# Seven-product chunks and the delays of deferred work set place by place, and the softmax reciprocal moved to the attended rows, in a hybrid decoder layer

## The chip, the cores and the metric

The kernel runs on one core of a Trainium2 chip. The metric is the device time of one execution in microseconds, and lower is better. The core has a matrix engine (TensorE, PE in the profile, with its weight loads as PEld), a vector engine (DVE), a scalar engine (ACT), GpSimd (POOL) and a synchronisation engine (SP), whose queue here issues nearly all DMAs.

## The reference

One decoder layer on 256 tokens of width 2048, in float32 (SEQ = 256, D_MODEL = 2048, N_MEM = 256, D_FF = 5632, 4 attention heads of 512):

```
hn = rmsnorm(h, norm_mix_w)
q, k, v, g_ret, xr, yr, g_a, g_b = split(hn @ w_in)
ret_out = silu(g_ret) * head_groupnorm(retention(rotary(q), rotary(k), v))
rnn_out = gelu(yr) * rg_lru(causal_dwconv(xr))
merged = sigmoid(g_a) * (ret_out @ w_proj_ret) + sigmoid(g_b) * (rnn_out @ w_proj_rnn)
h = h + merged @ w_mix_out
q = rmsnorm(h, norm_xa_w) @ xa_w_q;  k, v = mem_n @ xa_w_k, mem_n @ xa_w_v
h = h + (softmax(q k^T / sqrt(512)) v) @ xa_w_o              # per head
gate, val = split(causal_dwconv(rmsnorm(h, norm_ffn_w) @ w_up))
h = h + (silu(gate) * val) @ w_down
out = rmsnorm(h, final_norm_w)
```

Nearly all of the arithmetic lies in the weight products: a [256, K] activation times a [K, 512] block of columns, K being 2048 for most.

## The kernel before

**Weights.** `weight_plan` lists the weight products in their order. An entry is either one block of 512 columns or a pair of such blocks; a pair carries its own tuple from MARKS. `weight_stream` cuts them into chunks: a single block of 2048 rows has four chunks of 4 x 128 rows, a pair has eight chunks of 2 x 128 rows for both blocks. Each chunk is one 1 MB load into one of three `raw` buffers (RAW_BUFS), issued on SP. The chunks of a pair are numbered 0 to 7 here.

**Three products for one.** To hold float32 accuracy, every matrix is split into a high part and the rest. `weight_parts` does it for weights: ACT copies raw to `hi` (L355), DVE subtracts to `lo` (L356). Activations are split likewise (`split_pair`, `split_cols`). One product of 128x128x512 is then three matmuls, high x high, low x high and high x low. There are six buffers for each of hi and lo (PART_BUFS), and a tile holds two blocks of 128x512; a seven-product chunk takes four tiles of each, a plain pair chunk two. `chunks` runs `prefetch(AHEAD)`, so loads and splits are listed two chunks before the matmuls that use them.

**Seven products for eight.** A plain pair chunk multiplies a 2 x 2 arrangement (two halves of the tokens by two blocks of rows, two blocks of rows by two blocks of columns): eight block products, 24 matmuls. At the chunk positions named in MARKS the pair instead forms sums of the weight blocks (`seven_parts`, four additions on DVE, L376) and of the activations (`sums_of`, L454 to L465, kept for later products of the same activations until `token_sums` is cleared), and needs seven block products, 21 matmuls. Every pair has at least one such position before the change, mostly 2 and 5.

**Pair ends.** `steps_pair` accumulates in two acc and two sm banks of PSUM, in three more bank pairs for the seven-product chunks, and DVE adds them up at the end (L529, L540).

**Deferred work.** `later(n, fn)` puts fn into a list; `chunks` runs it n + 1 chunks on, after that chunk's matmuls have been listed. This is how the work between products gets its place: the transposes, rotary, retention, recurrence, softmax, convolutions, activation splits. `by_dma` turns rows into feature-major form: ACT copies the words to two planes (L562), SP issues transposing DMAs, and `join`, put off by `wait` chunks, copies the result back (L575) and calls `then`, which splits it for its reader.

**Order.** Matmuls stay in program order (`tc.keep_in_program_order`). For the other engines a scheduler at build time orders what is ready by its place in the program; `tc.high_priority(FREE)` moves evacuations of PSUM forward. So a later place in the program gives a lower rank behind weight splits.

**The order of products.** Retention: q, k, v and gates for four heads, twice (the gates as pairs, the second V as a pair). Recurrence: eight single products of w_in, then GB and w_proj_rnn, GA and w_proj_ret, w_mix_out. Attention: xa_w_k (two single blocks), two pairs of xa_w_q, a pair of xa_w_k, xa_w_v and xa_w_o (a pair and two single blocks each). Feed-forward: eleven blocks of w_up, each a pair of gate and value columns, in groups of 4, 4 and 3, with w_down of a group after the first block of the next one.

**Attention.** `softmax` takes the maximum, runs Exp with a summed output, and multiplies the probabilities by the reciprocal of the sum (L1090); `by_dma` turns them. `attend` multiplies by V, and `turned_rows` copies the result from PSUM (L586) for the next turn; with a scale r it multiplies instead (L588).

```python
def later(n, fn):
    pending.append((step[0] + n + 1, fn))
...
by_dma(rows, then, wait=1, pin=False)        # join put off by `wait` chunks
```

The functions that the change touches follow, with the line numbers that the profile uses.

Of the kernel before, what the change touches and what calls it, by code (L numbers as in the profile page):

```python
# [17 lines left out]
P = 128  # L18
# [10 lines left out]
BW = 512  # L29
# [7 lines left out]
RG_WAIT = 3  # L37
# [44 lines left out]
def weight_plan():  # L82
# [13 lines left out]
    plan += [("xa_w_k", 0, NT, 0), ("xa_w_k", 0, NT, BW), both("xa_w_q", 0), both("xa_w_q", 2 * BW), both("xa_w_k", 2 * BW)]  # L96
    plan += [both("xa_w_v", 0)] + [("xa_w_v", 0, NT, b * BW) for b in (2, 3)]
    plan += [both("xa_w_o", 0)] + [("xa_w_o", 0, NT, b * BW) for b in (2, 3)]
# [7 lines left out]
    marks = iter(one for stage in MARKS for one in stage)  # L106
    return [(*p[:3], (*p[3], next(marks)) if isinstance(p[3], tuple) else p[3]) for p in plan]


def marks_of(w, row=0):  # L110

    return next(c[2] for one, r, _, c in weight_plan() if (one, r) == (w, row) and isinstance(c, tuple))
# [59 lines left out]
def hybrid_layer(  # L172
# [308 lines left out]
    def steps_pair(w, row, st, nk, c1, c2):  # L481
# [15 lines left out]
        for k0, n, parts in chunks(nk, w, row, (c1, c2, seven)):  # L497
            k2 = k0 // KH
            for i in seven:
                if k2 < i <= k2 + 3 and (not isinstance(st, list) or i < len(st)):  # L500
                    sums_of(st[i])
# [42 lines left out]

    def product(o, l, r, start, stop):
# [33 lines left out]

    def turned_rows(a, r, then, wait=1, urgent=True):  # L580

        rows = big([P, 2, BW], s="rows")
        with tc.high_priority(FREE) if urgent else nullcontext():
            for tt in range(2):
                if r is None:
                    dve.tensor_copy(rows[:, tt, :], a[:, tt, :])  # L586
                else:
                    dve.tensor_scalar_mul(rows[:, tt, :], a[:, tt, :], r[:, tt : tt + 1])  # L588
# [169 lines left out]
    def retain(g, qr, kr, vs, dec, gates):  # L758
# [36 lines left out]
        def normalise():  # L795
# [18 lines left out]
            for i in range(2):  # L814
                later(2 * i, lambda i=i: two_heads(i))
# [107 lines left out]
    for b in range(4):  # L923
# [6 lines left out]
        def conv_x(f, b=b, xr=xr, wparts=wparts):  # L930
# [18 lines left out]
            for pr in range(2):  # L949
                later(RG_WAIT + pr, lambda pr=pr: both(pr))  # L950
# [10 lines left out]
        turned_rows(gemm_n("w_in", 0, xs, NT, O_YR + b * BW), rs0, gelu_y, 6)  # L961
# [25 lines left out]
    def turn_merged(f):  # L987
        for pr in range(2):
# [3 lines left out]
            if len(merged) == NT // 2:  # L992
                for i, k2 in enumerate(sorted(set(more) - set(marks))):
                    later(1 + i, lambda k2=k2: sums_of(merged[k2]))
            if len(merged) == 2:
                for k2 in range(NT // 2):
                    later(1 + 3 * k2, lambda k2=k2: ms[k2])

    ts, mb = [], []
    for b in range(2):  # L1000
        ts.append(tanh_rows(big([P, 2, BW], s="sig"), gemm_n("w_in", 0, xs, NT, O_GB + b * BW)))
        if b == 0:
            for i, k2 in enumerate(marks_of("w_proj_rnn")):
                later(1 + 2 * i, lambda k2=k2: sums_of(rnn[k2]))
# [14 lines left out]
    for b in range(4):  # L1019
        later(8 + b, lambda b=b: hrow.append(load_rows(x, b)))  # L1020
    for b in (0, 2):
        for i, m in enumerate(pair("w_proj_ret", 0, ret, NT, b * BW, (b + 1) * BW)):
            gated(ts[b + i], m)
            dve.tensor_add(m, m, mb[b + i])  # L1024
            by_dma(m, turn_merged, 1 + (b + i == 3))


    def residual(w, st, out, wcol, paired, marks):

        ss = sums()  # L1030
        products = [steps_n(w, 0, st, NT, b * BW) for b in range(4)]
        sources = []
        for b in range(4):
            if b in paired:
                sources += pair(w, 0, st, NT, b * BW, (b + 1) * BW)
            h = hrow[b]
            dve.tensor_add(h, h, sources.pop(0) if sources else ended(products[b]))
            by_dma(h, lambda f, b=b: turn(f, b, out, wcol, marks), 1 + (b % 2 if b in (*paired, *(i + 1 for i in paired)) else 0), b == 3 and w == "xa_w_o")
            if b < 2:
                later(2 + b, lambda h=h, b=b: squares(h, ss, b))  # L1040
# [20 lines left out]
    ss1 = residual("w_mix_out", merged, h1s, p_xa, (0, 2), ())  # L1061
# [5 lines left out]
    pTs, probs = [], []  # L1067
# [276 lines left out]
```

## Time and profile before

| quantity | value |
|---|---|
| median of 3 runs | 1971.8 us (1971.18 to 1973.38) |
| profiled execution | 1971.99 us, span 1970.2 us |
| TensorE matmuls | 8768, busy 1953.4 us (99%) |
| weight loads | busy 1618.3 us (82%) |
| DVE | 2190 instructions, busy 1653.1 us (84%) |
| ACT | 1729 instructions, busy 1417.8 us (72%) |
| weight loads by DMA | 352 of 1 MB, 4.9 us each from issue to landing |
| granted TensorE clock | 0.998 mean |

The profile is one execution. A stretch is given as start:end in us from the start of the span. "DVE lo L356" is the DVE instruction of line 356 that writes a tile `lo`; "A <- B" in a list of waits says that A was idle until B had ended. Busy times of an engine overlap with those of the others. Ends of matmuls are modelled, so their starts and counts say more than their busy share.

### The profile page before, as it was taken

What the parts mean: (1) busy time and instruction counts of PE and PEld (TensorE: products, weight loads), DVE (VectorE), ACT (ScalarE), POOL (GpSimd) and SP (SyncE); (2) the same over time, 40 slices, a digit from 0 to 9 for tenths busy, and PEclk for the clock granted to TensorE, in tenths of its full rate; (3) what the DMA queues carried; (4) which work ended last, traced back from release to release, by engine and by line L of the source; (5) the groups of instructions that cost most, each with busy time, mean ns of one, the idle gap of its engine ahead of it and who ended that gap; (6) DMA issues with size and microseconds to landing.
All of it is one profiled execution on the core that took longest, in us unless ns stands there. A gap on an engine that the chain in (4) does not pass through costs nothing.

```text
span 1970.2 us, 24139 instructions
## 1 busy us (share of the span) xinstructions
PE 1953.4 (99%) x8768; PEld 1618.3 (82%) x8768; DVE 1653.1 (84%) x2190; ACT 1417.8 (72%) x1729; POOL 31.9 (2%) x33
## 2 busy tenths in 40 slices
PE   9999999999999999999999999999999999999998
PEld 7888888888888888878888888888877888878887
DVE  6887987888798887997888767789999889998786
ACT  6666658999645666778678676888886578874783
POOL 0000001000000000000000000000000000000000
PEclk9999999999999999999999999999999999999999
DMA  8756567765555576678676656667667756767673
GB/s 333 241 214 168 191 244 211 213 224 193 194 213 191 192 262 231 225 237 255 210 212 216 208 176 211 219 210 227 211 208 226 268 195 219 230 209 256 219 245 119
DMA packets 198344, 429.82 MB, mean 218 GB/s; under 512 B 142160, under 2 KB 146768, under 8 KB 153168
## 3 DMA queue, kind: packets, MB, share of 16 engines
q1 hardware_dynamic: 197072, 424.09, 64.4%
q0 software_dynamic: 1152, 4.19, 1.1%
q8 instruction: 68, 1.11, 0.2%
q14 instruction: 52, 0.43, 0.1%
HBM read 388.39 MB, written 2.10 MB: 198 GB/s over the span
## 4 chain that ended last, share of the span: by engine, by line
PE 81%; DVE 10%; ACT 5%; issue 2%; DMA 2%; SPq 0%; POOL 0%; POOLq 0%; ACTq 0%; DVEq 0%
PE acc L257 56%; PE sm L257 24%; DVE lo L356 4%; ACT f L575 2%; ACT hi L355 2%; DMA raw<-in_wall 2%; DVE raw L376 1%; DVE fv L1158 1%; DVE o L540 1%; DVE o L529 1%; DVE s L596 0%; DMA pt<-pl 0%; DVE fo L1167 0%; ACT fg L1156 0%; ACT pl L562 0%
## 5 line engine op out<-in xcount | busy, mean ns | idle before, releaser
L356 DVE TENSOR_TENSOR lo<-raw,hi 128x1024 fp32r<-128x1024 f32 (+1 forms) x838 | 969.4, 1184 | 231.8 <-ACT hi L355 223.2
L355 ACT CAST hi<-raw 128x1024 fp32r<-128x1024 f32 (+1 forms) x838 | 824.3, 1014 | 391.0 <-DVE raw L376 108.0
L257 PE MATMUL acc<-hi,s 128*128 128x512 f32 (+1 forms) x3548 | 1087.3, 388 | 0.7 <-ACT hi L355 0.3
L257 PEld LDWEIGHTS acc<-hi,s 128*128 128x128 f32 x3548 | 663.2, 188 | 137.2 <-ACT hi L355 0.8
L257 PE MATMUL acc<-lo,s 128*128 128x512 f32 (+1 forms) x1774 | 687.4, 388 | 0.0
L257 PE MATMUL sm<-hi,s 128*128 128x512 f32 x1552 | 477.9, 389 | 0.0
L257 PEld LDWEIGHTS acc<-lo,s 128*128 128x128 f32 x1774 | 333.1, 188 | 68.7 <-DVE lo L356 0.4
L257 PEld LDWEIGHTS sm<-hi,s 128*128 128x128 f32 x1552 | 291.3, 188 | 60.6
L257 PE MATMUL sm<-lo,s 128*128 128x512 f32 x776 | 302.0, 389 | 0.0
L575 ACT COPY f<-pt 128x1024 uint16<-128x1024 uint16 x128 | 167.8, 1356 | 15.7 <-DMA pt<-pl 15.5
L376 DVE TENSOR_TENSOR raw<-raw 128x512 f32<-128x512 f32 x248 | 171.2, 690 | 4.3
L257 PEld LDWEIGHTS sm<-lo,s 128*128 128x128 f32 x776 | 145.7, 188 | 30.4 <-DVE lo L356 0.4
L257 PE MATMUL acc<-hi,ts 128*128 128x512 f32 x372 | 115.1, 390 | 1.2 <-ACT hi L355 1.2
L257 PEld LDWEIGHTS acc<-hi,ts 128*128 128x128 f32 x372 | 69.5, 188 | 16.6 <-ACT hi L355 2.6
L257 PE MATMUL acc<-lo,ts 128*128 128x512 f32 x186 | 73.8, 397 | 5.2 <-DVE lo L356 5.1
L562 ACT COPY pl<-o 128x1024 uint16<-128x1024 uint16 x64 | 62.2, 1040 | 5.9 <-DVE o L1024 5.2
L562 ACT COPY pl<-rows 128x1024 uint16<-128x1024 uint16 x44 | 43.8, 1042 | 17.7 <-DVE rows L586 10.3
L257 PEld LDWEIGHTS acc<-lo,ts 128*128 128x128 f32 x186 | 34.9, 188 | 17.0 <-DVE lo L356 10.2
L1158 DVE SCALAR_TENSOR_TENSOR fv<-f,pf,fv 128x255 f32<-128x255 f32 (+1 forms) x88 | 41.5, 483 | 3.3 <-ACT fv L1156 3.0
L529 DVE TENSOR_TENSOR o<-o,acc 128x512 f32<-128x512 f32 x64 | 43.7, 683 | 0.1
L540 DVE TENSOR_TENSOR o<-o,sm 128x512 f32<-128x512 f32 x64 | 42.7, 686 | 0.2
L540 DVE TENSOR_TENSOR o<-o,acc 128x512 f32<-128x512 f32 x64 | 41.1, 685 | 0.9 <-PE acc L257 0.8
(185 smaller groups left out, 1056.8 us busy)
## 6 DMA issues: line engine op xcount, KB each, us to landing
raw<-in_wall SPq DMA_DIRECT2D x352, 1024.0 KB, 4.9
nat<-in_x SPq DMA_DIRECT2D x8, 512.0 KB, 10.6
nat<-o POOLq DMA_DIRECT2D x8, 512.0 KB, 6.3
raw<-in_wall SPq DMA_DIRECT2D x7, 512.0 KB, 5.9
pt<-pl SPq DMA_TRANSPOSE x128, 3.3
nat<-in_mem SPq DMA_DIRECT2D x4, 512.0 KB, 6.8
xt<-in_x_t SPq DMA_DIRECT2D x3, 512.0 KB, 9.1
xt<-in_mem_t SPq DMA_DIRECT2D x3, 512.0 KB, 6.4
```

Of the source, the lines that this page charges most:

```text
L257: tc.keep_in_program_order(pe.matmul(*a, **k))
L355: act.copy(hi[:, cs], src[:, cs])
L356: dve.tensor_tensor(out=lo[:, cs], in0=src[:, cs], in1=hi[:, cs].bitcast(F32), op=ALU.subtract)
L376: dve.tensor_tensor(out=o, in0=a, in1=b, op=ALU.add)
L529: dve.tensor_tensor(out=o, in0=a, in1=b, op=op)
L540: dve.tensor_tensor(out=o, in0=o, in1=banks[a], op=ALU.add)
L562: act.copy(planes[:, tt], words[:, tt])
L575: act.copy(halves_[:, :, :, cs], turned_[:, :, :, cs])
L1158: dve.scalar_tensor_tensor(out=y[:, s:S], in0=z[:, j, 0 : S - s], scalar=pf[:, 2 - s, t : t + 1], in1=y[:, s:S], op0=ALU.mult, op1=ALU.add,)
```

## The change

It has three parts.

1. MARKS gets its own tuple for each pair. An empty tuple now makes `weight_plan` list two single blocks, which is how the first xa_w_k, the last xa_w_v and the last xa_w_o products stay single; `paired()` lets the code below ask which it is. The tuples name one to three chunk positions, among them neighbours such as (2, 5, 6).
2. LAG names the delay of each kind of deferred work. Some values are those of before (recur, two_heads, gelu, value), others differ: rnn 0 for 1, heads 7 for 4, squares 5 in steps of 1 for 6 in steps of 2, rows 12 for 8, merged 2 for 1, memory 3 for 1, merge_turn 2 for 1, turn 3 for 1, query_turn 3 and key_turn 4 for 1, attend 1 for 0, residual 3 for 2, gate 2 for 1. The two accumulating DMAs (acc_m, acc_h) are off at 0.
3. `softmax` leaves the probabilities unscaled and keeps the reciprocals in `shares`; `attend` gives them to `turned_rows`, which multiplies the attended rows on their way out of PSUM.

```diff
+LAG = dict(
+    sums=3, two_heads=2, recur=3, gelu=6, merged=2, memory=3, memory_step=3, rnn=0, rnn_step=2,
+    heads=7, heads_step=1, squares=5, squares_step=1, rows=12, rows_step=1, residual=3, gate=2,
+    value=4, merge_turn=2, query_turn=3, key_turn=4, turn=3, attend=1, acc_m=0, acc_h=0,
+)
...
 MARKS = [
-    ((2, 5), (5,), (2, 5)),
-    ((2, 5), (2, 5), (2, 5)),
-    ((2, 5), (2, 5), (2, 5), (2, 5)),
-    ((5,), (3, 5)),
-    ((2, 5), (2, 5), (2, 5), (2, 5)),
-    ((3, 5),),
-    ((2, 5), (2, 5), (2, 5), (2, 5), (2, 5), (2, 5), (2, 5)),
-    ((2, 5), (2, 5), (2, 5), (2, 5), (2, 5), (2, 5)),
-    ((2, 5), (2, 5)),
+    ((2, 5, 6), (3,), (3, 5, 6),),
+    ((2, 5), (2, 5, 6), (2, 5, 6),),
+    ((2, 4, 6), (2, 5), (2, 5), (5,),),
+    ((3,), (3, 5),),
+    ((), (2, 5), (2, 3), (2, 5), (2, 5), (),),
+    ((5, 6), (),),
+    ((2, 4), (2, 5), (5,), (2, 5), (2, 5), (2, 5), (2, 5),),
+    ((2, 3, 5), (5,), (2, 5), (2, 5), (2, 5), (2, 5),),
+    ((2, 5, 6), (3, 5),),
 ]
...
+            seven = next(marks)
+            out += [(w, row, nk, (*c, seven))] if seven else [(w, row, nk, one) for one in c]
...
         rows = big([P, 2, BW], s="rows")
             for tt in range(2):
-                if r is None:
-                    dve.tensor_copy(rows[:, tt, :], a[:, tt, :])
-                else:
-                    dve.tensor_scalar_mul(rows[:, tt, :], a[:, tt, :], r[:, tt : tt + 1])
+                dve.tensor_scalar_mul(rows[:, tt, :], a[:, tt, :], r[:, tt : tt + 1])
...
-                    later(1 + i, lambda k2=k2: sums_of(merged[k2]))
+                    later(LAG["merged"] + i, lambda k2=k2: sums_of(merged[k2]))
...
-                    later(1 + 3 * k2, lambda k2=k2: ms[k2])
+                    later(LAG["memory"] + LAG["memory_step"] * k2, lambda k2=k2: ms[k2])
...
-    later(4 + h, lambda h=h: split_head(h))
+    later(LAG["heads"] + LAG["heads_step"] * h, lambda h=h: split_head(h))
...
-    later(6 + 2 * c, lambda c=c: memory_squares(c))
+    later(LAG["squares"] + LAG["squares_step"] * c, lambda c=c: memory_squares(c))
...
-    later(8 + b, lambda b=b: hrow.append(load_rows(x, b)))
+    later(LAG["rows"] + LAG["rows_step"] * b, lambda b=b: hrow.append(load_rows(x, b)))
...
-            by_dma(m, turn_merged, 1 + (b + i == 3))
+            by_dma(m, turn_merged, LAG["merge_turn"] + (b + i == 3))
...
-            by_dma(h, lambda f, b=b: turn(f, b, out, wcol, marks), 1 + (b % 2 if b in (*paired, *(i + 1 for i in paired)) else 0), b == 3 and w == "xa_w_o")
+            by_dma(h, lambda f, b=b: turn(f, b, out, wcol, marks), LAG["turn"] + (b % 2 if two else 0), b == 3 and w == "xa_w_o")
...
         dve.reciprocal(rsm, sm)
-        for tt in range(2):
-            dve.tensor_scalar_mul(pr_[:, tt, :], pr_[:, tt, :], rsm[:, tt : tt + 1])
+        shares.append(rsm)
...
-            by_dma(a, lambda f, o=o: split_block(f, o), 1 + i)
+            by_dma(a, lambda f, o=o: split_block(f, o), LAG["key_turn" if w == "xa_w_k" else "query_turn"] + i)
...
-        turned_rows(a, None, lambda f: split_block(f, osp, marks_of("xa_w_o")))
+        turned_rows(a, shares[b], lambda f: split_block(f, osp, marks_of("xa_w_o")))
...
-        later(b, lambda b=b, v=v: attend(b, v))
+        later(LAG["attend"] + b, lambda b=b, v=v: attend(b, v))
...
-        for a, then, wait in zip(two, (gate, value), (1, wait)):
+        for a, then, wait in zip(two, (gate, value), (LAG["gate"], wait)):
```

More of the change, by code (lines that the diff above doesn't have):

```diff
@@ L36 @@
 FREE = 300
-RG_WAIT = 3
+LAG = dict(
[3 more added lines that the diff above has]
+)
 EPS = 1e-6
@@ L105, in weight_plan @@
             plan.append(both("ffn_w_up", a[0] * BW, apart=FF))
-    marks = iter(one for stage in MARKS for one in stage)
-    return [(*p[:3], (*p[3], next(marks)) if isinstance(p[3], tuple) else p[3]) for p in plan]
+    marks, out = iter(one for stage in MARKS for one in stage), []
+    for w, row, nk, c in plan:
+        if isinstance(c, tuple):
+            seven = next(marks)
+            out += [(w, row, nk, (*c, seven))] if seven else [(w, row, nk, one) for one in c]
+        else:
+            out.append((w, row, nk, c))
+    return out
 def marks_of(w, row=0):
-    return next(c[2] for one, r, _, c in weight_plan() if (one, r) == (w, row) and isinstance(c, tuple))
+    return next((c[2] for one, r, _, c in weight_plan() if (one, r) == (w, row) and isinstance(c, tuple)), ())
 def gate_up_at():
@@ L578, in by_dma, with scaled @@
         later(wait, join)
+    def scaled(a, r):
+        with tc.high_priority(FREE):
+            for tt in range(2):
+                act.mul(a[:, tt, :], a[:, tt, :], r[:, tt : tt + 1])
     def turned_rows(a, r, then, wait=1, urgent=True):
@@ L949, in conv_x @@
             for pr in range(2):
-                later(RG_WAIT + pr, lambda pr=pr: both(pr))
+                later(LAG["recur"] + pr, lambda pr=pr: both(pr))
         def gelu_y(f, xr=xr):
```

71 lines of the change are left out of this document (42 added, 29 removed).

## The prediction

> **What bounds the kernel now.** I read the page's engine shares first, then the busy time in stretches that begin with the first matmul of one weight product and end with the first of the next, then the waits, then the groups by form.
>
> ```profile
> span 1970.2 us, 24139 instructions
> PE 1953.4 (99%) x8768; PEld 1618.3 (82%) x8768; DVE 1653.1 (84%) x2190; ACT 1417.8 (72%) x1729; POOL 31.9 (2%) x33
> ```
>
> ```profile
> 500.00:600.00 100.00, 100.00 (x443) 82.81 (x442) 85.29 (x104) 55.85 (x62) 0.00 (x0) 1.00 0.51 190
> ```
>
> TensorE is the bound: in an undisturbed 100 us it starts 443 matmuls, so one costs 100/443 = 0.226 us. Time can go only by fewer matmuls or by removing the few places where TensorE waits. A product of eight chunks with two seven-product chunks has 8x24 - 2x3 = 186 matmuls, or 186 x 0.226 = 42.0 us; undisturbed ones below measure 42.2, and 42.8 with one such chunk. Anything longer is waiting. (Columns: stretch, length, then busy us of PE, PEld, DVE, ACT, POOL.)
>
> ```profile
> 92.90:135.10 42.20, 42.20 (x187) 34.82 (x186) 39.48 (x50) 23.75 (x27) 0.00 (x0) 1.00 0.60 215
> 185.90:230.10 44.20, 43.60 (x190) 35.21 (x189) 39.63 (x64) 34.72 (x40) 0.00 (x0) 1.00 0.71 214
> 230.10:272.30 42.20, 42.20 (x188) 34.96 (x187) 38.95 (x53) 22.81 (x27) 0.00 (x0) 1.00 0.59 218
> 550.90:593.10 42.20, 42.20 (x188) 34.95 (x187) 37.83 (x47) 22.48 (x26) 0.00 (x0) 1.00 0.55 199
> 593.10:635.20 42.10, 42.10 (x187) 34.87 (x186) 33.43 (x39) 22.46 (x26) 0.00 (x0) 1.00 0.55 198
> 635.20:677.40 42.20, 42.20 (x188) 34.93 (x187) 35.92 (x44) 23.25 (x28) 0.00 (x0) 1.00 0.50 186
> 761.70:805.20 43.50, 42.67 (x188) 34.79 (x187) 37.32 (x46) 31.72 (x38) 0.00 (x0) 1.00 0.72 243
> 805.20:848.00 42.80, 42.80 (x190) 35.44 (x189) 38.83 (x50) 31.76 (x39) 0.00 (x0) 1.00 0.73 245
> 848.00:892.70 44.70, 42.77 (x187) 34.76 (x186) 41.66 (x56) 35.66 (x51) 0.00 (x0) 1.00 0.66 214
> 1384.10:1426.90 42.80, 42.49 (x188) 34.85 (x187) 41.40 (x59) 36.86 (x46) 0.00 (x0) 1.00 0.65 221
> 1426.90:1470.60 43.70, 42.59 (x187) 34.66 (x186) 41.64 (x60) 38.33 (x48) 0.00 (x0) 1.00 0.67 217
> 1470.60:1514.60 44.00, 43.39 (x188) 34.54 (x187) 40.74 (x58) 35.39 (x44) 0.00 (x0) 1.00 0.69 215
> 1556.70:1598.90 42.20, 42.20 (x187) 34.92 (x187) 33.22 (x37) 21.62 (x24) 1.07 (x2) 1.00 0.69 232
> 1725.40:1769.00 43.60, 42.59 (x187) 34.74 (x186) 40.49 (x57) 36.38 (x46) 0.00 (x0) 1.00 0.71 217
> 1811.20:1853.40 42.20, 42.20 (x188) 34.95 (x187) 32.91 (x37) 21.64 (x24) 0.88 (x1) 1.00 0.67 226
> ```
>
> The losses are 44.2 - 42.8 = 1.4 (second V product), 43.5 - 42.2 = 1.3 (w_proj_ret, second pair), 44.7 - 42.2 = 2.5 (w_mix_out, second pair), 0.6 + 1.5 + 1.8 = 3.9 (blocks 3 and 4 of w_up, first w_down) and 1.4 (second w_down). Together 10.5 us. In the long ones DVE is busy for nearly all of it (41.64 of 43.7); in the two quiet ones it idles 9 us. So the deferred work on DVE, beside the weight splitting, sets these waits. The waits of the weight load agree:
>
> ```profile
> PEld acc L257 <- DVE lo L356: 10.6, 14, 1.5
> PEld acc L257 <- ACT hi L355: 3.3, 5, 1.6
> ...
> PEld sm L257 <- DVE o L540: 0.7, 1, 0.7
> PEld acc L257 <- DVE ps L1120: 0.7, 1, 0.7
> ```
>
> TensorE waits for the low parts of split weights, and twice in the attention stage for something else (at most 1.4 us together).
>
> **What a seven-product chunk and a token sum cost.**
>
> ```profile
> L356 DVE TENSOR_TENSOR lo<-raw,hi 128x1024 fp32r<-128x1024 f32 x770 | 926.1, 1227 | 230.3 <-ACT hi L355 221.7 <-PE acc L257 3.5
> L376 DVE TENSOR_TENSOR raw<-raw 128x512 f32<-128x512 f32 x248 | 171.2, 690 | 4.3
> L356 DVE TENSOR_TENSOR lo<-raw,hi 128x512 fp32r<-128x512 f32 x68 | 46.5, 688 | 1.5 <-ACT hi L355 1.5
> L454 DVE TENSOR_TENSOR g<-s 128x512 f32<-128x512 f32 x16 | 11.0, 687 | 0.1
> L460 DVE TENSOR_TENSOR tq<-g 128x256 f32<-128x256 f32 x16 | 6.8, 423 | 0.2
> L462 DVE TENSOR_TENSOR tq<-g,tq 128x128 f32<-128x128 f32 x16 | 4.6, 289 | 0.1
> L465 DVE TENSOR_TENSOR ts<-tq,ts 128x512 fp32r<-128x512 f32 x22 | 15.2, 689 | 1.4 <-ACT ts L464 1.4
> L586 DVE COPY rows<-acc 128x512 f32<-128x512 f32 x8 | 5.1, 685 | 1.2 <-PE acc L257 1.0
> L588 DVE TENSOR_SCALAR rows<-acc,ro 128x512 f32<-128x512 f32 x28 | 19.7, 744 | 5.1 <-PE acc L257 5.1
> L1090 DVE TENSOR_SCALAR prob<-prob,sx 128x256 f32<-128x256 f32 x8 | 2.5, 351 | 0.1
> ```
>
> ```profile
> L355 ACT CAST hi<-raw 128x1024 fp32r<-128x1024 f32 x770 | 785.1, 1049 | 372.7 <-DVE raw L376 108.0 <-PE sm L257 105.8 <-DMA raw<-in_wall 78.3
> ```
>
> A plain pair chunk takes 2 x 1.227 = 2.45 us of DVE and 24 matmuls, a seven-product one 4 x 0.690 + 3 x 1.227 + 0.688 = 7.13 us and 21. So each buys 3 x 0.226 = 0.68 us of TensorE for 4.68 us of DVE. The 248 additions of L376 are four each: 62 such chunks. Counted from the new MARKS there are 66. A chunk position that is new for its activations also needs a token sum: 0.687 + 0.423 + 2 x 0.289 (L462 and its twin) + 0.689 = 2.38 us of DVE. There are 22 (L465); the new places make 31.
>
> **The change part by part**, against the profiled execution (1971.99 us, its span and 1.8 around it; 0.2 above the median of the runs shown).
>
> 1. Matmuls: 4 more such chunks remove 12, 12 x 0.226 = **-2.7 us**. (The Trainium skill, "TensorE: Matmul & The Clock Gate", Back-to-back issue gap, gives about 131 ns per matmul of this width when weight loads are pipelined with them: 1.6 us instead, as an estimate. The trace's spacing of 226 ns disagrees, and decides.)
>
> 2. Second half of the mixer: the second w_proj_ret product loses chunk 2, the first w_mix_out product moves its one from chunk 5 to 3, and the turns and splits of merged and memory tiles come one to two chunks later, which takes DVE work out of 848.0 to 892.7. DVE gains 4.68 us against a loss of 1.3 + 2.5 = 3.8.
>
> ```profile
> ACT hi L355 <- DMA raw<-in_wall: 5.6, 4, 2.9
> ```
>
> But in 848.0 to 892.7 the casts also wait 5.6 us for weights, whose issue queues on SP behind other transfers, and the loads of x rows now come four chunks later past weight loads on that queue (still a whole product ahead of their first reader). I take **-2.8** (0 to -3.8).
>
> 3. First feed-forward half: block 2 of w_up drops chunk 2, just ahead of the 3.9 us lost. DVE gains 4.68, TensorE's own time there grows by 0.68, one token sum (new chunk 4 in block 0) takes 2.38 back: net 2.98 of lead. **-3.0** (0 to -3.9).
>
> ```profile
> L575 ACT COPY f<-pt 128x1024 uint16<-128x1024 uint16 x128 | 167.8, 1356 | 15.7 <-DMA pt<-pl 15.5
> ```
>
> The last turn of xa_w_o is joined two chunks later, with two chunks left to its reader (21 + 24 matmuls, 10.2 us). Ahead of that reader stand on ACT its two copies, 2.7 us, and at most six casts of 1.049 for the weights of those chunks, 6.3: 9.0 in all, with its own splits behind. It just fits: 0, at most +2, once. Gate joins one chunk later; its reader waits for value anyway: 0.
>
> 4. Second half: block 6 drops chunk 2; block 5 gains one with a sum, 7.06 us, where 42.2 - 33.2 = 9.0 us are idle. The 1.4 us go: **-1.4** (0 to -1.4).
>
> 5. Second V product: its chunk moves from 5 to 3 and asks a new sum, 2.38 us, in a stretch already short. **-0.4** (-1.4 to +2.4).
>
> 6. Attention: probabilities lose 8 x 0.351 = 2.8 us, attended rows pay 8 x (0.744 - 0.685) = 0.5 on DVE; attend, keys and queries come one to three chunks later. The attended rows wait for a reciprocal finished many chunks before. Of the 1.4 us I take **-0.5** (-1.4 to +1.4, as much again).
>
> 7. Added chunks, extra DVE against idle DVE: 92.9: 7.06 to 2.7; 230.1: 4.68 to 3.3 (sums made before); 550.9: 7.06 to 4.4; 593.1: 7.06 to 8.7; 635.2: 7.06 to 6.3; 1811.2: 7.06 to 9.3. Short are 4.4 + 1.4 + 2.7 + 0.8 = 9.3 us, which must come out of the lead that the splitting has. That lead shows where casts wait for TensorE to free a part buffer, here in 593.1 to 635.2 and in 92.9 to 135.1:
>
> ```profile
> ACT hi L355 <- PE sm L257: 10.0, 8, 1.7
> ```
>
> ```profile
> ACT hi L355 <- PE sm L257: 4.7, 4, 1.7
> ```
>
> As long as they wait, splitting is as far ahead as six buffers allow. So nearly all is covered: **+0.7** (0 to 9.3), nearer the first end because no such wait of TensorE stands in these stretches now.
>
> 8. Moves of work alone. The splits of heads come three chunks later, the loads and squares of memory rows up to four chunks earlier (past weight loads on SP), two token sums one chunk earlier, two squares of the residual one later. The branches on paired() leave the same products single as before, and recur, two_heads, gelu and value keep their delays: 0.
>
> ```profile
> 677.40:719.50 42.10, 42.10 (x187) 34.89 (x186) 40.42 (x58) 31.50 (x45) 0.24 (x1) 1.00 0.75 272
> ```
>
> ```profile
> L622 DVE SCALAR_TENSOR_TENSOR s<-f,pb,s 128x256 fp32r<-128x256 f32 x48 | 21.2, 481 | 5.4 <-ACT s L621 5.4
> ```
>
> At most three more heads (2 x 0.481 each) and one more of their token sums enter this stretch: 2.9 + 2.4 = 5.3 us of DVE on 1.7 idle. All heads still end before their reader: **0**, the lead taking it (0 to +3.6).
>
> Sum: -2.7 - 2.8 - 3.0 - 1.4 - 0.4 - 0.5 + 0.7 = -10.1, so 1971.99 - 10.1 = **1961.9 us** (-0.5%). With every term at its good end: -2.7 - 3.8 - 3.9 - 1.4 - 1.4 - 1.4 = -14.6, 1957.4.
>
> **The rivals.**
>
> *The loss only moves.* DVE gets 4 x 4.68 + 9 x 2.38 - 2.3 = 37.8 us more in all (1653 to about 1691). If what it saves in the saturated stretches is used up by the next saturated one, only the matmuls stay: 1971.99 - 2.7 = 1969.3. For it: the losses stand in a row (0.6, 1.5, 1.8), a backlog carried on. Against: each removal lies just ahead of its backlog and is larger than it.
>
> *Back-to-back chunks outrun the splitting: slower.* Eight products now have two seven-product chunks side by side (5, 6 or 2, 3). Such a pair needs 14.3 us of DVE while TensorE runs 42 matmuls, 9.5 us, and eight part buffers of six. Without lead each costs 14.3 - 9.5 = 4.8 us. Four lie where DVE is short or the deferred work dense (both gate products of retention, the second query product, xa_w_o): 4 x 4.8 = 19.2, 1961.9 + 19.2 = 1981. It decides from a little over two such pairs (10.1/4.8). Against: the second chunk's third part can be cast once TensorE is six matmuls into the first (1.4 us), takes 1.049 + 1.227 = 2.3, and is read 30 matmuls in (6.8 us), so 3.1 us are spare. (The Trainium skill, "Perfetto Trace Analysis", Optimization Strategy, holds that the same gap repeating on a saturated engine can mean too few buffers for the next tile; by it these pairs would show such a gap, and this rival is what it makes here. No stretch of the trace has such a pair, so the trace cannot yet say.)
>
> **How the numbers follow.** The forecast has 0.70, the moving loss 0.14, the slower rival 0.16. A measurement of this kernel tells about 0.2% (3.9 us) from no change: the forecast is faster, the moving loss (-0.14%) within, the third slower. The range is 1957 (all terms good) to 1975 (two or three uncovered pairs), leaving out most of the slower rival. The forecast's own range is 1957 to 1967.
>
> **What would show it.** 8756 matmuls, L376 x264 and ts x31; DVE near 1690 us. The w_up blocks 3 and 4 and the first w_down at 42.2 us each, w_mix_out's second pair near 43. The weight load's wait for low parts falls from 10.6 to under 4 us. The gate products with chunks 5 and 6 last 41.5 us (183 matmuls); 46 would mean the slower rival. Wrong would be also a new wait at the first w_up product's chunk 6, for the late turn, or tile slots running out where a third token sum is held through the feed-forward.

## The result and the profile after

The changed kernel takes 1964.54 us (median of 6 runs, 1962.38 to 1965.87); the kernel before took 1971.92 us in 6 runs beside it (1969.63 to 1973.38). The ratio is 0.9962, with a 95% interval of 0.9949 to 0.9975: 7.4 us or 0.38% faster. The profiled execution took 1962.41 us, 9.6 less than the profiled one of before. A second sample of the same kernel on another chip, taken with the last experiments, had a median of 1964.81 us and a ratio of 0.9949 (0.9936 to 0.9961).

Line numbers of the changed kernel are 9 higher in the product code (the cast L355 is now L364, the low part L356 is L365, the matmul L257 is L266); further down the shift grows, and the rows from PSUM are at L604.

First the page of the changed kernel, its span and its engine shares:

```profile
span 1960.6 us, 24200 instructions
PE 1947.5 (99%) x8756; PEld 1616.5 (82%) x8756; DVE 1683.2 (86%) x2251; ACT 1426.2 (73%) x1746; POOL 35.2 (2%) x33
```

There are 12 matmuls fewer, and DVE has 30 us more to do. Next its stretches, each from the first matmul of a weight product to the first of the next, with the same columns as in the prediction: the first gate product of retention, the second V product, the second gate product, the second pair of w_proj_ret, the two pairs of w_mix_out, w_up blocks 3 and 4, the first w_down, and the two pairs of the second w_down.

```profile
92.10:133.60 41.50, 41.50 (x185) 34.27 (x184) 41.16 (x57) 24.88 (x30) 0.00 (x0) 1.00 0.51 188
184.30:227.50 43.20, 43.20 (x191) 35.35 (x190) 41.72 (x62) 35.58 (x42) 0.00 (x0) 1.00 0.74 232
227.50:269.00 41.50, 41.50 (x185) 34.37 (x184) 40.52 (x63) 23.52 (x27) 0.00 (x0) 1.00 0.55 200
756.40:799.20 42.80, 42.80 (x191) 35.43 (x190) 36.88 (x46) 29.22 (x33) 0.00 (x0) 1.00 0.72 244
799.20:842.00 42.80, 42.80 (x190) 35.45 (x189) 40.33 (x50) 32.80 (x40) 0.00 (x0) 1.00 0.82 272
842.00:884.20 42.20, 42.20 (x188) 34.93 (x187) 38.21 (x50) 35.40 (x50) 0.00 (x0) 1.00 0.67 221
1375.10:1417.30 42.20, 42.20 (x188) 34.91 (x187) 37.95 (x54) 35.52 (x45) 0.00 (x0) 1.00 0.68 223
1417.30:1459.60 42.30, 42.30 (x187) 34.83 (x186) 40.87 (x60) 37.24 (x47) 0.00 (x0) 1.00 0.65 224
1459.60:1503.60 44.00, 42.68 (x187) 34.75 (x186) 41.36 (x58) 37.42 (x47) 0.00 (x0) 1.00 0.66 215
1714.40:1757.20 42.80, 42.61 (x187) 34.54 (x186) 39.73 (x54) 34.99 (x43) 0.00 (x0) 1.00 0.71 221
1757.20:1800.90 43.70, 42.56 (x187) 34.93 (x187) 39.98 (x48) 21.45 (x24) 1.73 (x2) 1.00 0.73 244
```

The products with three such chunks last 41.5 us, those with two 42.2, those with one 42.8: what 183, 186 and 189 matmuls take. So the second half of the mixer runs without a wait now, and w_up blocks 3 and 4 nearly so. The first w_down (44.0) is as slow as before, and the second w_down still waits.

The waits of the changed kernel's weight load (total us, times, longest):

```profile
PEld acc L266 <- DVE lo L365: 4.0, 8, 1.7
PEld acc L266 <- DVE s L612: 1.9, 2, 1.0
PEld sm L266 <- issue: 1.5, 1, 1.5
...
PEld acc L266 <- ACT s L611: 0.8, 1, 0.8
```

The wait for low parts has fallen from 10.6 to 4.0 us. The second and the last row (L611 and L612 split the hidden tiles of the feed-forward) belong to the last w_down, where TensorE waits for the last hidden tiles. The third stands at the start of the second pair of the second w_down; the matmuls there wait 1.1 us for L549, the closing additions of the pair before.

For one measure in all runs I summed, over the matmuls of a product, what the distance from one start to the next exceeds the undisturbed 226.7 ns; where small jitter is cut off moves such a sum by about 0.1. The table gives these waits in us; the changed kernel has two columns, for its two profiled executions.

| place | before | changed | changed, second sample |
|---|---|---|---|
| second V product | 1.4 | 0.3 | 0.3 |
| second pair of w_proj_ret, w_mix_out | 3.9 | 0 | 0 |
| attention (xa_w_v, xa_w_o) | 1.2 | 0 | 0 |
| w_up blocks 3 and 4, first w_down | 4.0 | 2.0 | 2.2 |
| w_up block 8, second w_down | 1.5 | 2.2 | 2.2 |
| last w_down | 0.7 | 2.3 | 4.9 |
| first product of the kernel | 3.3 | 2.4 | 3.4 |

The last two rows move by 2.6 and 1.0 us between two executions of one kernel; the others stay within 0.2. In the second sample a pause in the last w_down is longer (2.4 us over the undisturbed spacing, for 0.7), and the granted clock falls behind it, as the last section shows. The first execution lies at the low end of its six runs, which is why the profiles differ by 9.6 us and the medians by 7.4.

### The profile page after: what moved, and what is told of

Read it like the earlier page. It is cut to its first block, busy times and chain, and to the rows that moved or that the text cites. A ratio compares the mean times of both kernels' runs of the same rounds, so it can differ in the third digit from the quotient of the medians.

```text
span 1960.6 us, 24200 instructions
## 1 busy us (share of the span) xinstructions
PE 1947.5 (99%) x8756; PEld 1616.5 (82%) x8756; DVE 1683.2 (86%) x2251; ACT 1426.2 (73%) x1746; POOL 35.2 (2%) x33
## 4 chain that ended last, share of the span: by engine, by line
PE 91%; DVE 4%; ACT 2%; issue 1%; DMA 1%; POOL 0%; POOLq 0%; DVEq 0%; SPq 0%; ACTq 0%
PE acc L266 63%; PE sm L266 28%; DVE lo L365 2%; DMA raw<-in_wall 1%; ACT hi L364 1%; DVE fv L1185 0%; DVE o L538 0%; ACT f L588 0%; DVE raw L385 0%; ACT pl L575 0%; DVE fo L1194 0%; ACT o L1311 0%; DVE o L549 0%; DMA raw<-in_head 0%; DVE fg L1185 0%
## 5 line engine op out<-in xcount | busy, mean ns | idle before, releaser
L365 DVE TENSOR_TENSOR lo<-raw,hi 128x1024 fp32r<-128x1024 f32 (+1 forms) x846 | 973.9, 1178 | 190.1 <-ACT hi L364 182.9
L364 ACT CAST hi<-raw 128x1024 fp32r<-128x1024 f32 (+1 forms) x846 | 829.4, 1012 | 368.3 <-DVE raw L385 109.6
L266 PE MATMUL acc<-hi,s 128*128 128x512 f32 (+1 forms) x3540 | 1085.1, 388 | 1.6 <-DVE s L612 1.1
L266 PEld LDWEIGHTS acc<-hi,s 128*128 128x128 f32 x3540 | 661.5, 188 | 138.1 <-DVE s L612 1.9
L266 PE MATMUL acc<-lo,s 128*128 128x512 f32 (+1 forms) x1770 | 686.2, 388 | 1.3 <-DVE lo L365 1.3
L266 PE MATMUL sm<-hi,s 128*128 128x512 f32 x1520 | 468.1, 389 | 1.1 <-DVE o L549 1.1
L266 PEld LDWEIGHTS acc<-lo,s 128*128 128x128 f32 x1770 | 332.3, 188 | 70.8 <-DVE lo L365 2.5
L266 PEld LDWEIGHTS sm<-hi,s 128*128 128x128 f32 x1520 | 285.2, 188 | 60.8 <-issue 1.5
L266 PE MATMUL sm<-lo,s 128*128 128x512 f32 x760 | 295.7, 389 | 0.0
L385 DVE TENSOR_TENSOR raw<-raw 128x512 f32<-128x512 f32 x264 | 181.4, 687 | 4.0
L266 PEld LDWEIGHTS sm<-lo,s 128*128 128x128 f32 x760 | 142.7, 188 | 29.6
L266 PE MATMUL acc<-hi,ts 128*128 128x512 f32 x396 | 121.9, 389 | 0.0
L266 PEld LDWEIGHTS acc<-hi,ts 128*128 128x128 f32 x396 | 74.3, 188 | 15.4
L266 PE MATMUL acc<-lo,ts 128*128 128x512 f32 x198 | 77.4, 391 | 0.2 <-DVE lo L365 0.2
L1311 ACT ACTIVATE o<-o,ro 128x512 f32<-128x512 f32 x44 | 30.1, 718 | 20.0 <-DVE o L549 19.5
L266 PEld LDWEIGHTS acc<-lo,ts 128*128 128x128 f32 x198 | 37.1, 188 | 9.0 <-DVE lo L365 1.5
L538 DVE TENSOR_TENSOR o<-o,acc 128x512 f32<-128x512 f32 x64 | 43.5, 680 | 0.5
L1185 DVE SCALAR_TENSOR_TENSOR fg<-f,pf,fg 128x255 f32<-128x255 f32 (+1 forms) x88 | 39.1, 478 | 4.5 <-ACT fg L1183 4.2
L549 DVE TENSOR_TENSOR o<-o,sm 128x512 f32<-128x512 f32 x64 | 42.3, 678 | 0.2
```

The costliest lines, as they stand in the source:

```text
L266: tc.keep_in_program_order(pe.matmul(*a, **k))
L364: act.copy(hi[:, cs], src[:, cs])
L365: dve.tensor_tensor(out=lo[:, cs], in0=src[:, cs], in1=hi[:, cs].bitcast(F32), op=ALU.subtract)
L385: dve.tensor_tensor(out=o, in0=a, in1=b, op=ALU.add)
L538: dve.tensor_tensor(out=o, in0=a, in1=b, op=op)
L549: dve.tensor_tensor(out=o, in0=o, in1=banks[a], op=ALU.add)
```

## Experiments

The expectations name their theories by letters. The kernels ran in three batches, each on one chip, with the kernel before beside it: 1973.85 us (30 runs) for the three parts alone and `gate1`; 1974.41 (12 runs) for `close_in_ffn`, `three_in_a_row`, `mixer_delays_old` and `last_blocks_old`; 1974.64 (9 runs) for `turn1`, `loads_old`, `fewer_at_ends` and `after_again`. Times are compared across batches by their ratio to that. Unless said otherwise, an edit is shown against the changed kernel.

### The three parts alone

`marks_only` has the new MARKS; LAG gets the delays of before, and softmax scales the probabilities as before.

```diff
-    sums=3, two_heads=2, recur=3, gelu=6, merged=2, memory=3, memory_step=3, rnn=0, rnn_step=2,
-    heads=7, heads_step=1, squares=5, squares_step=1, rows=12, rows_step=1, residual=3, gate=2,
-    value=4, merge_turn=2, query_turn=3, key_turn=4, turn=3, attend=1, acc_m=0, acc_h=0,
+    sums=3, two_heads=2, recur=3, gelu=6, merged=1, memory=1, memory_step=3, rnn=1, rnn_step=2,
+    heads=4, heads_step=1, squares=6, squares_step=2, rows=8, rows_step=1, residual=2, gate=1,
+    value=4, merge_turn=1, query_turn=1, key_turn=1, turn=1, attend=0, acc_m=0, acc_h=0,
...
-        shares.append(rsm)
+        for tt in range(2):
+            dve.tensor_scalar_mul(pr_[:, tt, :], pr_[:, tt, :], rsm[:, tt : tt + 1])
+        shares.append(None)
```

> The new positions alone, all delays and the softmax as before. Theory A (the positions carry the gain, because they take vector work away just ahead of a backlog): 12 matmuls fewer (-2.7 us), the mixer's 3.8 us of waits down to about 1, the first feed-forward half's 3.9 down to about 2: 1964 to 1966 us. Theory B (the delays carry it, the positions only cost vector time): the waits stay near 10.5 us and only the matmuls go, 1969 us or more.

Measured: 1971.62 us (12 runs, 1969.05 to 1974.32), ratio 0.9987 (0.9977 to 0.9996).

`lag_only` has the new delays with the MARKS and the softmax of before.

```diff
-    ((2, 5, 6), (3,), (3, 5, 6),),
+    ((2, 5), (5,), (2, 5)),
...
-        shares.append(rsm)
+        for tt in range(2):
+            dve.tensor_scalar_mul(pr_[:, tt, :], pr_[:, tt, :], rsm[:, tt : tt + 1])
+        shares.append(None)
```

> The new delays alone, positions and softmax as before (8768 matmuls). Theory A: only the mixer and the attention stage gain, 1 to 2 us, and the second w_down and the last w_down lose 1 to 2 as in the full change: 1970 to 1972 us. Theory B: the full change less the matmuls, about 1967 us.

Measured: 1973.92 us (12 runs), ratio 1.0002 (0.9994 to 1.0011).

`softmax_only` moves the reciprocal and leaves MARKS and delays as before. Against the kernel before, its edit in `softmax` is this:

```diff
-        for tt in range(2):
-            dve.tensor_scalar_mul(pr_[:, tt, :], pr_[:, tt, :], rsm[:, tt : tt + 1])
+        shares.append(rsm)
```

> The reciprocal at the attended rows alone. Theory A: 2.3 us of vector work less in a stage where TensorE lost at most 1.1 us: 1971 to 1972 us. Rival: the chain from the probabilities to the value products was what TensorE waited for, and all 1.1 us go: 1970.7 us.

Measured: 1974.81 us (10 runs), ratio 1.0000 (0.9991 to 1.0010).

The waits of the three, in us:

| place | positions alone | delays alone | softmax alone | all |
|---|---|---|---|---|
| second V product | 0.35 | 2.1 | 2.3 | 0.3 |
| second w_proj_ret, w_mix_out | 3.2 | 2.6 | 3.9 | 0 |
| attention | 0.2 | 1.3 | 0.6 | 0 |
| w_up 3 and 4, first w_down | 4.5 | 4.1 | 4.7 | 2.0 |
| w_up 8, second w_down | 3.1 | 4.0 | 1.0 | 2.2 |
| last w_down | 2.5 | 1.4 | 0.8 | 2.3 |

Alone the parts give -0.13%, 0 and 0; together they give -0.38% (second sample -0.51%). The gain is in the combination. The positions alone save what their 12 matmuls cost (2.2 us of a possible 2.7). They do nearly empty the second V product and the attention stage. In the mixer they leave 3.2 us of 3.9, the delays alone leave 2.6, both together leave none; in the first feed-forward half either alone leaves all of it. So the theory that freeing DVE just ahead of a backlog is enough to clear it, on which the forecast rested, falls.

### Gate one chunk earlier

`gate1` is the changed kernel with the delay of the gate columns as before.

```diff
-    heads=7, heads_step=1, squares=5, squares_step=1, rows=12, rows_step=1, residual=3, gate=2,
+    heads=7, heads_step=1, squares=5, squares_step=1, rows=12, rows_step=1, residual=3, gate=1,
```

> The changed kernel with the gate's delay back at 1. Theory C (the late gate pushes convolution work into the ends of the blocks, and so made the new waits in both first w_down products, the second w_down pair and the last w_down): the 1.9 + 0.6 + 1.5 + 2.3 us there fall by half or more, about 1961 us by the median. Rival D (the new waits come from the added positions of blocks 5, 9 and 10, which leave less lead and hold a third token sum): no change, about 1964.5 us.

Measured: 1967.92 us (5 runs, 1967.20 to 1968.52), ratio 0.9967 (0.9954 to 0.9979). This interval overlaps that of the changed kernel, so the time says little; the trace says more. The waits are 5.9 us in w_up blocks 3 and 4 and the first w_down (2.0 and 2.2 in the two executions of the changed kernel) and 3.5 in block 8 and the second w_down (2.2 in both). The seven traces that have these positions and the later gate (two of the changed kernel, five of the kernels below) wait 2.0 to 3.8 and 1.0 to 2.6 us there. So the idea that the later gate costs time in the second half finds no support: the earlier gate waits longer, though that is one trace, and the times do not tell the two apart.

Where the difference stands, shows in w_up blocks 1 to 4 taken as one stretch. First the changed kernel, busy time of the stretch, then the wait of DVE's low parts in it:

```profile
1290.10:1459.60 169.50, 169.50 (x748) 140.13 (x748) 155.46 (x224) 145.14 (x179) 0.00 (x0) 1.00 0.65 213
```

```profile
DVE lo L365 <- ACT hi L364: 12.6, 12, 2.2
```

The same two views of `gate1`, and from the second also the wait of the weight load:

```profile
1290.00:1463.50 173.50, 170.88 (x749) 139.68 (x748) 156.12 (x226) 147.11 (x181) 0.00 (x0) 1.00 0.63 209
```

```profile
DVE lo L365 <- ACT hi L364: 16.2, 11, 2.9
...
PEld acc L266 <- DVE lo L365: 4.4, 5, 1.5
```

DVE does the same work in both (155.5 and 156.1 us), in 169.5 and 173.5 us. It idles 16.2 - 12.6 = 3.6 us more behind the casts of ACT, close to the 4.0 us by which the stretch is longer. That it idles more follows from equal work in a longer stretch; that it idles behind the casts is what the trace adds. With the positions alone the same idle time is 14.6 us, in 172.0 us. The step from a join of gate and value work that falls together on ACT to casts that come late is inferred from these sums; no run moved a single ACT instruction, so why the casts come late stays open.

### Neighbouring positions where the work is dense, and three in a row

`close_in_ffn` gives w_up blocks 3, 4 and 7 the neighbours (5, 6) instead of (2, 5); the matmuls stay the same in number.

```diff
-    ((2, 4), (2, 5), (5,), (2, 5), (2, 5), (2, 5), (2, 5),),
-    ((2, 3, 5), (5,), (2, 5), (2, 5), (2, 5), (2, 5),),
+    ((2, 4), (2, 5), (5,), (5, 6), (5, 6), (2, 5), (2, 5),),
+    ((2, 3, 5), (5,), (5, 6), (2, 5), (2, 5), (2, 5),),
```

> The changed kernel with chunks 5, 6 instead of 2, 5 in blocks 3, 4 and 6+1 of w_up (block 6 keeps its one), where vector work is dense; same number of matmuls and token sums but one. Theory (the lead pays for neighbours, nothing else): lead at chunk 5 grows by the 4.7 us that chunk 2 no longer takes, so a pair costs 0 to 2 us each, at most 1970 us. Slower rival of the prediction (4.8 us for each pair where vector work is dense): three pairs, 14 us, 1979 us.

Measured: 1980.79 us (9 runs), ratio 1.0033 (1.0024 to 1.0043). Against the ratios of the changed kernel (0.9962 and 0.9949) that is 0.71 to 0.84%, 14 to 17 us for three pairs, about 5 each. Blocks 3, 4 and 7 in this kernel, which take 42.2 us undisturbed:

```profile
1376.00:1426.40 50.40, 43.26 (x187) 34.49 (x185) 44.03 (x65) 39.20 (x49) 0.00 (x0) 1.00 0.66 215
1426.40:1470.70 44.30, 44.14 (x187) 36.10 (x188) 38.28 (x55) 34.93 (x43) 0.00 (x0) 0.96 0.57 182
1640.00:1687.40 47.40, 43.17 (x188) 34.38 (x186) 39.51 (x57) 36.63 (x46) 0.00 (x0) 1.00 0.67 211
```

They lose 8.2, 2.1 and 5.2 us. The largest wait is not for a weight. Its waits between 1403 and 1428 us:

```profile
PEld acc L266 <- DVE o L538: 5.5, 1, 5.5
PE acc L266 <- DVE o L538: 5.1, 1, 5.1
```

L538 adds a product's sums in PSUM to the output at the end of a pair, and so frees the banks of the next product. Ahead of it in DVE's timeline stand low parts and token sums with hardly a gap, and the first addition of L538 also needs ACT's copy L531, which ran behind the token sum's cast L473 (start, length):

```profile
1422.62 1.22 DVE L365 TENSOR_TENSOR lo<-raw,hi 128x1024 fp32r<-128x1024 f32 x1
1423.76 0.28 DVE L471 TENSOR_TENSOR tq<-fo,tq 128x128 f32<-128x128 f32 x1
1423.96 1.22 DVE L365 TENSOR_TENSOR lo<-raw,hi 128x1024 fp32r<-128x1024 f32 x1
1425.10 0.68 DVE L474 TENSOR_TENSOR ts<-tq,ts 128x512 fp32r<-128x512 f32 x1
1425.70 0.68 DVE L538 TENSOR_TENSOR o<-o,acc 128x512 f32<-128x512 f32 x1
```

```profile
1424.07 0.62 ACT L473 CAST ts<-tq 128x512 fp32r<-128x512 f32 x1 [1.04 <-DVE tq L471]
1424.60 0.58 ACT L531 COPY o<-acc 128x512 f32<-128x512 f32 x1
```

A queue of late DVE work thus holds up the end of a product as well as its weights. The edit does two things at once: (5, 6) for (2, 5) makes neighbours, and it moves the last seven-product chunk, and with it the closing additions, from chunk 5 to chunk 6. No run separates the two, so the 5 us are the price of both.

`three_in_a_row` puts neighbours where DVE has time: chunks 4, 5, 6 in the second GB product, the second w_proj_rnn and w_up block 9.

```diff
-    ((2, 5), (2, 5, 6), (2, 5, 6),),
+    ((2, 5), (4, 5, 6), (4, 5, 6),),
...
-    ((2, 5, 6), (3, 5),),
+    ((4, 5, 6), (3, 5),),
```

> Chunks 4, 5, 6 instead of 2, 5, 6 in the second GB product, the second w_proj_rnn product and block 9 of w_up, all quiet. Theory (only lead pays): three take 21.4 us of vector time against 14.3 of TensorE, 7.1 us, and the lead before chunk 4 is about 8 us, so 0 to 1 us of waiting in each stretch. By the rule that too few buffers make a gap that repeats, each stretch would show the same gap, 2 us or more, at chunks 5 and 6.

Measured in one run: 1969.59 us, span 1967.8. The three products and, last, the GA product after the first two:

```profile
548.60:590.10 41.50, 41.50 (x184) 34.26 (x183) 39.40 (x53) 22.11 (x25) 0.00 (x0) 1.00 0.46 167
590.10:631.70 41.60, 41.60 (x185) 34.28 (x184) 40.40 (x54) 24.72 (x29) 0.00 (x0) 1.00 0.56 203
1805.30:1846.90 41.60, 41.60 (x185) 34.29 (x184) 34.87 (x42) 21.19 (x23) 1.74 (x2) 1.00 0.60 205
631.70:675.20 43.50, 42.03 (x184) 34.26 (x183) 41.73 (x51) 23.62 (x29) 0.00 (x0) 1.00 0.61 227
```

The products with three neighbours take 41.5 to 41.6 us: no wait at all. The price appears in the next product, 43.5 against 41.5 undisturbed, and 3.2 us more in the first 5 us of the last w_down, two products after block 9, where no other trace pauses. From the trace's starts and ends I worked out how far ahead of the weight load that needs it a low part ends. In block 9 that is 8.1 us for the third part of chunk 4, 2.9 for that of chunk 5, 0.7 for that of chunk 6, and next to nothing (0.1) for the second part of chunk 7. The other two products agree, but for 6.4 us at chunk 4 of w_proj_rnn. A chunk of this kind takes lead, and whoever comes when none is left pays.

(The Trainium skill, "Perfetto Trace Analysis", Optimization Strategy, says that one gap repeating on the engine that should be saturated can mean too few buffers. By it these neighbours, which ask for eight part buffers of six, would each show a gap; the three stretches at 41.5 to 41.6 us do not bear that out. Here the question is lead, and it is paid elsewhere.)

### Which delays matter in the mixer

Three kernels take a few delays back in the changed kernel. `mixer_delays_old`:

```diff
-    sums=3, two_heads=2, recur=3, gelu=6, merged=2, memory=3, memory_step=3, rnn=0, rnn_step=2,
+    sums=3, two_heads=2, recur=3, gelu=6, merged=1, memory=1, memory_step=3, rnn=0, rnn_step=2,
...
-    value=4, merge_turn=2, query_turn=3, key_turn=4, turn=3, attend=1, acc_m=0, acc_h=0,
+    value=4, merge_turn=1, query_turn=3, key_turn=4, turn=3, attend=1, acc_m=0, acc_h=0,
```

> The changed kernel with merged, memory and merge_turn back at 1. Theory E (neither the positions nor the delays alone clear a backlog; together they do): w_proj_ret's second pair and both w_mix_out pairs, 0 us of waits in the changed kernel, wait 2 to 3.5 us again, the rest as it is: about 1967 us. Rival (the delays of heads, squares, rows and turn, which stay, did it): still 0 there, 1964.5 us.

Measured: 1963.63 us (4 runs), ratio 0.9942 (0.9926 to 0.9959); the mixer waits 0.3 us.

`turn1`:

```diff
-    value=4, merge_turn=2, query_turn=3, key_turn=4, turn=3, attend=1, acc_m=0, acc_h=0,
+    value=4, merge_turn=2, query_turn=3, key_turn=4, turn=1, attend=1, acc_m=0, acc_h=0,
```

> The changed kernel with the residual's turn joined one chunk on again instead of three (after w_mix_out and after xa_w_o). Theory F (of the delays it is this one that cleared w_mix_out: its copies and splits stood on the scalar engine ahead of the casts of w_mix_out's second pair): 2 to 3 us of waits return there, about 1967 us. Rival G (the loads of x rows did, by queueing ahead of weight loads): 0 stays.

Measured: 1964.59 us (4 runs), ratio 0.9953 (0.9936 to 0.9969); the mixer waits 0, the first feed-forward half 3.7 us instead of 2.0, w_up block 0 another 0.6.

`loads_old`:

```diff
-    heads=7, heads_step=1, squares=5, squares_step=1, rows=12, rows_step=1, residual=3, gate=2,
+    heads=4, heads_step=1, squares=6, squares_step=2, rows=8, rows_step=1, residual=3, gate=2,
```

> The changed kernel with heads, squares and rows at their delays of before. Rival G: 2 to 3 us of waits return in w_proj_ret's second pair and w_mix_out. Theory F: 0 stays there, within 1 us.

Measured in one run: 1964.93 us, span 1963.1; the mixer waits 0.5 us.

None of these brings back more than 0.5 of the 3.2 us that the positions alone leave there. Which delay clears the mixer stays open: several may each suffice, or it is residual or rnn, which were not tried. The delay of turn, too, seems to help the first feed-forward half, though 1.7 us in one execution of each is thin.

### Fewer positions ahead of each w_down

`last_blocks_old` gives w_up blocks 9 and 10 their positions of before.

```diff
-    ((2, 5, 6), (3, 5),),
+    ((2, 5), (2, 5),),
```

> The changed kernel with chunks 2, 5 again in blocks 9 and 10 of w_up: 3 matmuls more (+0.7 us). Theory (the added vector work there took the lead that the last w_down needs): its wait, 2.3 us, falls to 0.7 to 1.4, so about 1963.8 us. Rival (the later gate delays the last hidden tiles, whatever the positions): 2.3 us stay, 1965.2 us.

Measured: 1962.78 us (4 runs, 1961.20 to 1964.08), ratio 0.9936 (0.9921 to 0.9951). The last w_down waits 0.6 us instead of 2.3 or 4.9, with three matmuls more. All traces bear this out: 2.3 to 4.9 us in the eight that have the new positions in blocks 9 and 10, 0.6 to 1.4 in the five that have (2, 5) in both.

That and the waits left in both other w_downs led to `fewer_at_ends`: one position each taken out of blocks 4, 8 and 9, just ahead of the w_downs, 8765 matmuls, nine more than in the changed kernel (9 x 0.2267 = 2.0 us).

```diff
-    ((2, 4), (2, 5), (5,), (2, 5), (2, 5), (2, 5), (2, 5),),
-    ((2, 3, 5), (5,), (2, 5), (2, 5), (2, 5), (2, 5),),
-    ((2, 5, 6), (3, 5),),
+    ((2, 4), (2, 5), (5,), (2, 5), (5,), (2, 5), (2, 5),),
+    ((2, 3, 5), (5,), (2, 5), (5,), (2, 5), (2, 5),),
+    ((2, 5), (2, 5),),
```

> The changed kernel with one position less in the last block of each group that w_down follows (blocks 4, 8: chunk 5 alone; blocks 9, 10: 2, 5): 9 matmuls more, +2.0 us. Theory (what TensorE still waits for at both w_down products and the last one is vector work carried over from those blocks): 1.9 + 2.2 + 2.3 us fall to about 1 in all, 3.4 us better than the changed kernel on the same chip. Rival (these waits come from the order at the block's end and not from the amount): they stay, and it is 2 us worse.

`after_again` is the changed kernel unaltered, on the same chip.

> The changed kernel once more, beside the others on the same chip: the ratio of 0.996 to the kernel before again, and the waits stretch by stretch within 1 us of the first profile (1.9 in the first w_down pair, 2.2 in the second w_down, 2.3 in the last).

Measured: `fewer_at_ends` 1960.74 us (5 runs, 1960.02 to 1962.28), ratio 0.9928 (0.9916 to 0.9941); `after_again` 1964.81 us (5 runs, 1962.97 to 1966.20), ratio 0.9949 (0.9936 to 0.9961). The ranges do not meet: 4.1 us less, and the best of all the kernels here. The page of `fewer_at_ends`:

```profile
span 1958.4 us, 24177 instructions
PE 1948.6 (100%) x8765; PEld 1618.6 (83%) x8765; DVE 1669.3 (85%) x2228; ACT 1422.3 (73%) x1739; POOL 36.5 (2%) x33
```

Its w_up blocks 3 and 4, its first w_down and the first pair of the second:

```profile
1375.40:1417.60 42.20, 42.20 (x188) 34.94 (x187) 37.96 (x54) 35.52 (x45) 0.00 (x0) 1.00 0.69 224
1417.60:1460.40 42.80, 42.80 (x190) 35.45 (x189) 39.38 (x57) 36.09 (x45) 0.00 (x0) 1.00 0.66 221
1460.40:1502.60 42.20, 42.20 (x188) 34.94 (x187) 37.93 (x53) 36.56 (x45) 0.00 (x0) 1.00 0.68 224
1714.10:1757.10 43.00, 42.77 (x188) 34.64 (x187) 38.48 (x55) 35.72 (x45) 0.00 (x0) 1.00 0.70 221
```

The first w_down goes from 44.0 to 42.2 us, for 0.5 more in block 4; in the nine traces that have (2, 5) in block 4 and the other positions of the changed kernel up to there, the first w_down waits 1.7 to 2.2 us. At the second w_down the proof is weaker: 0.9 us here, but the seven traces named at `gate1` span 1.0 to 2.6 without any change of position. Over the three places the feed-forward waits 0 + 0.9 + 1.2 us, where the two executions of the changed kernel waited 2.0 + 2.2 + 2.3 and 2.2 + 2.2 + 4.9. More matmuls and less time: the last positions had cost more than they saved, at the first and the last w_down for certain.

## Why the prediction was right, and where it was not

The direction and the range held, and the forecast of 1961.9 lies 2.6 us under the median. The effect was 7.4 us by the medians where 10.1 were forecast. The bound, the price of a matmul and, within 8 us, the amount of DVE work were right; why the waits went was only half right. By the two profiled executions, of which the second lies at the low end of its runs, the terms came out so:

| step of the prediction | forecast | measured |
|---|---|---|
| 1 matmuls | -2.7 | -2.7 |
| 2 second half of the mixer | -2.8 | -3.9 |
| 3 first feed-forward half | -3.0 | -2.0 |
| 4 second half | -1.4 | +0.7 |
| 5 second V product | -0.4 | -1.1 |
| 6 attention | -0.5 | -1.2 |
| 7 added chunks | +0.7 | 0 in their products |
| 8 moves of work alone | 0 | 0 |
| last w_down, named by no step | 0 | +1.6 |
| first product, end of the kernel | 0 | -1.0 |
| sum | -10.1 | -9.6 |

That the sums lie so close is in part luck: five rows came out better than forecast, by 4.2 us together, and three worse, by 4.7.

**Step 1** is exact: 8756 matmuls. The groups by form of the changed kernel give the additions, the token sums and the scaled attended rows as counted:

```profile
L385 DVE TENSOR_TENSOR raw<-raw 128x512 f32<-128x512 f32 x264 | 181.4, 687 | 4.0
L474 DVE TENSOR_TENSOR ts<-tq,ts 128x512 fp32r<-128x512 f32 x31 | 21.2, 683 | 0.7 <-ACT ts L473 0.7
...
L604 DVE TENSOR_SCALAR rows<-acc,sx 128x512 f32<-128x512 f32 x8 | 5.6, 745 | 1.3 <-PE acc L266 1.3
```

DVE has 1683 us in place of the forecast 1691.

**Step 2** had the right sign and was too small, and its reasoning was half of the cause: `marks_only` leaves 3.2 us there and `lag_only` 2.6. Removed work and later work are both needed.

**Step 3** is the step whose reasoning failed. It balanced amounts of DVE work (a net lead of 2.98 us) and costed the gate's later join at 0. The amounts alone left 4.5 us, and the gate's delay, worth 0 in the sum, was worth 3.9 of waiting by one trace (5.9 to 2.0), in which DVE idles longer behind ACT's casts. What went is the wait of blocks 3 and 4 (2.2 us, now 0.2); the first w_down, forecast at 42.2 us, stayed at 44.0, and in `fewer_at_ends`, with a position less in block 4, it is 42.2. The late turn of xa_w_o, feared at up to +2, cost nothing.

**Step 4** did not come true, and in the changed kernel it had the wrong sign. What dropping chunk 2 of block 6 gave did not carry to the second w_down, three products later. The step counted on weights alone, but the larger part of the wait there, 1.5 of 2.2 us, is the second pair waiting for the closing additions of the first. How much the positions matter here stays open: other kernels with the same positions in these blocks wait 1.0 to 2.6 us.

**Steps 5 and 6** came out larger by 0.7 each. The same second V product waited 1.4, 2.1 and 2.3 us in three kernels whose positions there are those of before, so part of it is scatter; with the new position all eleven traces show 0.3 to 0.4.

**Step 7** costed the added chunks in the products that hold them, and there they cost less than forecast. Its error was the place: the positions of blocks 9 and 10 took time that the last w_down was short of. `last_blocks_old` shows this (0.6 us there), without telling the two blocks apart, and `three_in_a_row` shows such a shift at another place. In the changed kernel it is the hidden tiles that come late there, not the weights. This is the term the sum lacked.

**The slower rival** priced a neighbouring pair without lead at 4.8 us; `close_in_ffn` measures about 5 where the work is dense. So its price came near, partly by luck, as the largest wait there is for closing additions and not for split weights. Its condition was not met: the pairs of the change lie where lead covers them, at 41.5 us for a product with three such chunks. **The rival in which the loss only moves** is what the positions do alone: -2.2 us.

## What to carry to other kernels

When an engine feeds a saturated one through a few buffers, count lead, not busy time: extra work is free where lead is left, and its bill can come one or two products later, so look there before calling it free. Work that is deferred matters by when it falls on the engine ahead of the bottleneck's feeder (here, it seems, ACT's casts ahead of DVE's low parts), and two edits that give nothing alone can give the gain together. Before adding the last few savings, take some out again where a backlog stands next: nine matmuls more made this kernel 4.1 us faster.

## What the hardware showed beside

The wait of 5.1 us in `close_in_ffn` cost more than itself. The stretches behind it (the column before the last two is the granted clock):

```profile
1426.40:1428.40 2.00, 1.97 (x5) 1.59 (x6) 2.00 (x3) 0.00 (x0) 0.00 (x0) 0.50 0.79 332
1428.40:1430.40 2.00, 2.00 (x8) 1.57 (x7) 2.00 (x4) 1.63 (x2) 0.00 (x0) 0.67 0.88 254
1430.40:1433.50 3.10, 3.10 (x15) 2.58 (x14) 2.52 (x4) 3.10 (x6) 0.00 (x0) 1.00 0.86 259
```

TensorE's granted clock was 0.50 for the first 2 us after the pause and 0.67 on average in the next 2: 11 matmuls started in 4.0 us, where 17 or 18 fit. So the pause cost about 1.5 us more (4.0 - 11 x 0.227). The waits of 0.5 to 1.5 us in the changed kernel left the clock at 1.00. Shorter pauses than 5.1 us can do the same, though: in `after_again` TensorE idled 2.1 us at the pause in the last w_down, and behind it:

```profile
1922.10:1925.40 3.30, 3.01 (x7) 1.69 (x7) 3.19 (x4) 1.57 (x2) 0.00 (x0) 0.50 0.68 283
```

In `lag_only`, too, 2.1 us of idle TensorE in block 8 are followed by 3.2 us at 0.50 (1685.2 to 1688.4), a part of its 4.0 us there, while 1.6 us idle in `gate1`, in the last w_down, left the clock at 1.00. (The Trainium skill, "TensorE: Matmul & The Clock Gate", Part 1: The HAM clock gate, says that after some 3.4 us without work the clock falls to half, and that as long a busy stretch releases it. The traces agree on the release: if the clock went straight from 0.50 to 1.00, a mean of 0.67 puts full speed some 3.3 us after the first matmul. On the pause they agree for 5.1 us, but 2.1 us were enough twice here, and the measurement decides.)
